# GpSimd makes the w2 sums of M1 and M3 one stage earlier, w2 tiles lie in column halves, and the M6/M7 differences overwrite g

## The chip, the cores and the metric

The kernel runs on one core of a Trainium2 chip. The metric is the device time of one execution in microseconds (us). It is measured over several executions on the chip; a profile of one execution gives a trace. The core has TensorE (PE; its weight loads are listed apart as PEld), VectorE (DVE), ScalarE (ACT), GpSimd (POOL) and SyncE (SP), whose queue here only issues DMAs.

## The reference, cut to what matters

```python
x  = randn(8, 1024, 1024); w1 = randn(1024, 4096); w2 = randn(4096, 1024)   # float32
h = x @ w1
h = 0.5 * h * (1 + np.tanh(np.sqrt(2 / np.pi) * (h + 0.044715 * h ** 3)))
out = (h @ w2).astype(np.float32)
```

## The kernel before

The 8192 rows are worked off in eight superblocks (sb 0 to 7) of 1024 rows. In each, the *first matmul* is x @ w1 with the activation, which leaves g in SBUF as four quarter blocks (g11, g12, g21, g22), and the *second matmul* is g @ w2. Each is a Strassen-like scheme: the operands are cut into 2 x 2 blocks and seven products M1 to M7 of sums and differences replace eight block products. The second matmul's products multiply these:

```python
B_TERMS = {1: ("11", SUB, "22"), 2: ("11", None, None), 3: ("12", ADD, "22"), 4: ("21", ADD, "11"),
           5: ("22", None, None), 6: ("11", ADD, "12"), 7: ("21", ADD, "22")}      # of w2
A_TERMS = {1: ("11", "22"), 2: ("21", "22"), 3: ("11", None), 4: ("22", None),
           5: ("12", "11"), 6: ("21", "11"), 7: ("12", "22")}                       # differences of g
```

A product can be run *one-level* (64 TensorE matmuls of 512 columns) or *two-level*: the same scheme is applied again inside the product, and 7 x 16 matmuls of 256 columns replace the 64. Two-level needs, besides the product's own operand of w2 (4 tiles), its four inner w2 sums. They are made once, stored to DRAM (`in_d`), and loaded by every later superblock. Superblocks 0 and 1 run everything one-level and store the sums of M2, M6 and M7. Superblock 2 runs M2, M6 and M7 two-level, and its second matmul makes the sums of M1 and M3 on VectorE while those products run one-level. Superblocks 3 to 7 run M1, M2, M3, M6 and M7 two-level, and M4 and M5 one-level.

What VectorE does between the products is a table; a key such as `51` means "after step 1 of M5":

```python
FILL_END = """;50:x621 x622;51:x611 a61;52:x612 a62;53:a63 a64
    ;61:x721;62:x722;63:x711;64:a71;65:x712;66:a72;67:a73
    ;71:a74;72:n5;73:n1;74:n2;75:n7;76:n6"""
FILL_2 = (
    dict(inner=(1, 2, 3, 6, 7), fill=slots("""00:x122 x112 a11 a12 a13 a14 x222 x212 ...""" + FILL_END)),
    dict(inner=(2, 6, 7), fill=slots("""00:g10 g11 g12 g13 x222 x212          # superblock 2
    ;10:a21 s11;11:a22 s12;12:a23 s13;13:a24 s14 s15
    ... ;30:s31;31:s32;32:s33;33:s34 s35""" + FILL_END)),
)
# x621: block 21 of M6's difference of g;  a61: M6's inner sum 1;  g10: M1's one-level difference;
# s11..s14: M1's inner w2 sums, s15: store plain quarters of M1's w2;  n5: a difference for the next x
```

`unit()` takes one of the 26 buffers (4 KB in each partition) that nearly everything shares: w1 and w2 tiles, differences, output sums.

```python
up = ctx.enter_context(tc.tile_pool(name="up", bufs=26))

def split_jobs(m, pieces):                     # inner w2 sums of product m
    ...
    def make(n):
        j, u, op, v = W_SUMS[n]
        t[n] = unit(NI // 2, OH // 2)
        for h in range(2):
            tt(t[n][:, h * QC:(h + 1) * QC, :], operand(u, h), operand(v, h), op, True)   # VectorE
        nc.gpsimd.dma_start(out=in_d[m][:, j - 1], in_=t[n])
    def plain():                               # the three quarters that are no sums: copied to DRAM
        for j, b in W_TERMS.items():
            for h in range(2):
                nc.gpsimd.dma_start(out=in_d[m][:, j - 1, h * QC:(h + 1) * QC, :], in_=operand(b, h))

class Inner:                                   # a two-level product
    def load(self):
        for j in W_ORDER:
            self.y[j] = unit(NI // 2, OH // 2)
            nc.sync.dma_start(out=self.y[j], in_=in_d[self.m][:, j - 1])
    def make_x(self, b):
        self.x[b] = unit(NI // 2, HT // 2)
        tt(self.x[b], inner_block(self.u, b), inner_block(self.v, b), SUB, True)

def matmul2(sb, g, early, nxt):
    order = (4, 1, 2, 3, 5, 6, 7)              # M4 first, M7 last
    ...
```

Output sums and M-products go to DRAM by DMAs that GpSimd issues; until such a store has read its tile, the tile's buffer is not free.

## Time and profile before

| | |
|---|---|
| time, 3 runs | median 1538.98 us (1538.09 to 1539.83) |
| span of the profiled run | 1538.1 us |
| TensorE busy | 1523.8 us, 99% |
| first matmul of sb 2, of sb 3 | 96.8, 96.7 us |
| second matmul of sb 2 | 99.5 us |
| second matmul of sb 3 to 6 | 89.1 us each |

TensorE is busy for 99% of the span, so only its own work and the gaps between its work matter. From the page of the kernel before, the busy times of the engines (us, share of the span, instructions):

```profile
PE 1523.8 (99%) x8606; PEld 844.5 (55%) x8606; DVE 1071.2 (70%) x1354; ACT 489.3 (32%) x821; POOL 330.7 (21%) x380
```

The windows view of the kernel before, cut at the stage boundaries that the chain of waits shows; the rows are the first and second matmul of superblock 2, then of superblock 3. Columns: the stretch, its length, then busy time and instructions of each engine, the granted clock of TensorE (1.00 is full), the DMA engines' mean busy share, and GB/s:

```profile
409.24:506.00 96.76, 96.76 (x450) 43.86 (x448) 57.41 (x84) 45.81 (x79) 16.45 (x20) 1.00 0.74 232
506.00:605.48 99.48, 94.16 (x593) 58.57 (x592) 69.41 (x82) 14.05 (x24) 29.66 (x43) 0.98 0.94 318
605.48:702.17 96.69, 96.69 (x449) 43.83 (x448) 55.18 (x81) 45.79 (x79) 22.61 (x18) 1.00 0.75 215
702.17:791.25 89.08, 88.92 (x690) 67.31 (x688) 72.66 (x82) 11.71 (x20) 16.43 (x21) 1.00 1.00 323
```

The two first matmuls are alike. Superblock 2's second matmul is 10.4 us longer than superblock 3's. Its TensorE is idle for 99.48 - 94.16 = 5.3 us, its mean clock is 0.98, and the rest of the difference is the one-level M1 and M3.

TensorE's timeline of that second matmul, from M5 on (start us, length, what; in brackets the idle time before it and who ended it):

```profile
559.50 13.98 PE L764 MATMUL ps<-u,gc 128*128 128x512 f16 x64
573.37 1.92 PE L699 MATMUL ps<-u 128*128 128x256 f16 x16
577.37 1.92 PE L699 MATMUL ps<-u,gc 128*128 128x256 f16 x16 [2.08 <-DVE gc L146]
579.13 1.91 PE L699 MATMUL ps<-u 128*128 128x256 f16 x16
581.97 3.65 PE L699 MATMUL ps<-u,gc 128*128 128x256 f16 x32 [0.93 <-DVE u L146]
585.46 1.91 PE L699 MATMUL ps<-u 128*128 128x256 f16 x16
589.68 2.78 PE L699 MATMUL ps<-u,gc 128*128 128x256 f16 x16 [2.31 <-DVE u L146]
592.25 2.75 PE L699 MATMUL ps<-u 128*128 128x256 f16 x16
594.84 1.91 PE L699 MATMUL ps<-u,gc 128*128 128x256 f16 x16
```

16 matmuls of 256 columns take 1.75 us start to start when nothing waits (as from 577.37 to 579.13); this is the *pitch*. The three marked groups start 4.00, 2.84 and 4.22 us after the group before them: 2.25, 1.09 and 2.47 us late, 5.8 us together. After the third, two groups of 16 take 2.57 and 2.59 us instead of 1.75: 1.7 us more. The windows view around it shows why:

```profile
587.00:590.40 3.40, 1.09 (x11) 0.83 (x9) 3.40 (x5) 0.00 (x0) 0.00 (x0) 1.00 1.02 414
590.40:594.00 3.60, 3.60 (x20) 2.60 (x19) 3.60 (x5) 0.00 (x0) 1.49 (x2) 0.53 0.86 281
594.00:597.00 3.00, 3.00 (x29) 2.70 (x28) 1.62 (x3) 0.59 (x1) 0.95 (x1) 1.00 0.99 191
```

From 590.4 to 594.0 the granted clock was 0.53 on average. What VectorE was doing before those gaps, from its timeline:

```profile
563.77 0.69 DVE L146 TENSOR_TENSOR u<-u,ps 128x512 f32<-128x512 f32 x1 [1.51 <-ACT tmp L159]
569.22 2.36 DVE L146 TENSOR_TENSOR u<-g,g 128x2048 f16<-128x2048 f16 x2 [4.76 <-DMA out_dram<-u]
...
573.23 1.22 DVE L146 TENSOR_TENSOR gc<-u 128x2048 f16<-128x2048 f16 x1
...
584.93 2.36 DVE L146 TENSOR_TENSOR u<-g,g 128x2048 f16<-128x2048 f16 x2 [3.02 <-DMA out_dram<-u]
587.21 0.68 DVE L146 TENSOR_TENSOR u<-tmp,ps 128x512 f32<-128x512 f32 x1
```

It sat idle for 4.76 us, and again for 3.02 us, until an output store had landed, and then made M6's and, from 584.93 on, M7's differences (`u<-g,g`), each in a buffer of its own. The inner sums (`gc<-u`) and the sum that empties a PSUM bank (`u<-tmp,ps`), for which TensorE waited, came after them in VectorE's order.

In the later superblocks one small gap is left in each second matmul. From the waits view of TensorE over superblocks 3 to 7:

```profile
PE ps L699 <- DVE u L146: 0.8, 5, 0.2
```

### The profile page before, as it was taken

The page shows a single profiled execution, that of the slowest core. Times are in us where ns is not written, and L with a number is a line of the kernel's source. Part 1 is how long each engine was busy: PE and PEld are TensorE (multiplying, and loading weights), DVE is VectorE, ACT ScalarE, POOL GpSimd, SP SyncE. Part 2 cuts the span into 40 slices and gives each one's busy share as a digit, 9 for nine tenths or more (in the row PEclk, how much of TensorE's full clock was granted, in tenths as well). Part 3 has the DMA queues.
Part 4 walks back from the last instruction along what each step waited for, and adds up shares of the span by engine and source line. Part 5 has one row for each costly group of instructions (what it writes and reads, how often), then busy time and mean ns, then how long its engine had stood idle before and what let it go on. Part 6 is the DMA issues. An engine that isn't in the chain of part 4 may idle for free.

```text
span 1538.1 us, 22679 instructions
## 1 busy us (share of the span) xinstructions
PE 1523.8 (99%) x8606; PEld 844.5 (55%) x8606; DVE 1071.2 (70%) x1354; ACT 489.3 (32%) x821; POOL 330.7 (21%) x380
## 2 busy tenths in 40 slices
PE   9999999999999999999999999999999999999998
PEld 5444444444444556446774467644775448744486
DVE  6876868768755567556875568755786566965677
ACT  6645024410244211442124421244113441144300
POOL 1242011212302241140211302122121310204011
PEclk9999999999999999999999999999999999999999
DMA  9999985994966799868997599966999669993696
GB/s 321 344 326 348 248 276 186 316 309 157 372 210 198 254 375 307 261 171 284 329 306 225 159 350 304 320 192 194 335 319 306 185 212 323 313 339 97 216 335 175
DMA packets 212654, 415.19 MB, mean 270 GB/s; under 512 B 77376, under 2 KB 84544, under 8 KB 211648
## 3 DMA queue, kind: packets, MB, share of 16 engines
q1 hardware_dynamic: 178560, 307.29, 59.2%
q0 software_dynamic: 33984, 106.45, 25.3%
q8 instruction: 67, 1.10, 0.3%
q14 instruction: 43, 0.35, 0.1%
HBM read 304.09 MB, written 124.26 MB: 278 GB/s over the span
## 4 chain that ended last, share of the span: by engine, by line
PE 90%; DMA 5%; DVE 2%; issue 1%; SPq 1%; ACT 0%; POOL 0%; DVEq 0%; POOLq 0%; ACTq 0%
PE ps L367 48%; PE ps L764 22%; PE ps L699 20%; DMA out_dram<-u 2%; DMA gc<-in_w_dram 2%; DVE u L146 1%; SPq L156 1%; DVE gc L146 1%; DMA u<-in_d 0%; DVE tmp L146 0%; DMA u<-in_x_dram 0%; ACT u L181 0%; POOL u L162 0%; ACT g L377 0%; POOL out_dram L478 0%
## 5 line engine op out<-in xcount | busy, mean ns | idle before, releaser
L367 PE MATMUL ps<-u 128*128 128x512 f16 x3584 | 776.2, 379 | 3.3 <-DVE tmp L146 1.7
L367 PEld LDWEIGHTS <-u 128*128 128x128 f16 x3584 | 350.5, 98 | 426.8 <-issue 4.9
L146 DVE TENSOR_TENSOR tmp<-tmp,ps 128x512 f32<-128x512 f32 x528 | 361.9, 687 | 296.4 <-ACT tmp L431 113.0
L377 ACT ACTIVATE g<-tmp 128x512 f16<-128x512 f32 x256 | 161.2, 630 | 293.6 <-DVE tmp L146 293.3
L764 PE MATMUL ps<-u,gc 128*128 128x512 f16 x1088 | 236.6, 379 | 0.0
L146 DVE TENSOR_TENSOR u<-u 128x2048 f16<-128x2048 f16 (+3 forms) x245 | 221.5, 933 | 15.8 <-ACT u L322 11.7
L699 PE MATMUL ps<-u,gc 128*128 128x256 f16 x1792 | 210.2, 273 | 6.1 <-DVE u L146 4.0
L699 PEld LDWEIGHTS <-gc 128*128 128x128 f16 x1792 | 175.6, 98 | 28.1 <-issue 5.3
L377 ACT ACTIVATE g<-ps 128x512 f16<-128x512 f32 x256 | 151.6, 596 | 88.7 <-PE ps L367 88.3
L764 PEld LDWEIGHTS <-gc 128*128 128x128 f16 x1088 | 106.4, 98 | 127.4
L764 PE MATMUL ps<-u,g 128*128 128x512 f16 x704 | 153.7, 379 | 0.0
L699 PE MATMUL ps<-u 128*128 128x256 f16 x1104 | 132.6, 274 | 0.0
L159 ACT COPY tmp<-ps 128x512 f32<-128x512 f32 x56 | 32.8, 586 | 274.0 <-PE ps L699 151.8
L146 DVE TENSOR_TENSOR u<-u,ps 128x512 f32<-128x512 f32 x129 | 88.4, 685 | 43.1 <-ACT tmp L159 19.1
L699 PEld LDWEIGHTS <-u 128*128 128x128 f16 x1104 | 108.4, 98 | 15.7 <-DVE u L146 0.4
L490 POOL DMA_DIRECT2D out_dram<-u x54 | 55.6, 1038 | 282.4 <-DVE u L146 263.3
L764 PEld LDWEIGHTS <-g 128*128 128x128 f16 x704 | 68.9, 98 | 82.9
L469 POOL TENSOR_TENSOR u<-g,g 128x2048 f16<-128x2048 f16 x22 | 89.2, 4065 | 81.7 <-ACT g L377 60.1
L431 ACT COPY tmp<-ps 128x512 f32<-128x512 f32 x128 | 72.9, 570 | 70.4 <-PE ps L367 69.7
L478 POOL DMA_DIRECT2D out_dram<-u x56 | 41.2, 764 | 240.8 <-ACT u L159 212.2
L146 DVE TENSOR_TENSOR tmp<-ps,tmp 128x512 f32<-128x512 f32 x128 | 88.4, 691 | 5.9 <-PE ps L367 1.2
L146 DVE TENSOR_TENSOR u<-g,g 128x2048 f16<-128x2048 f16 x70 | 83.5, 1220 | 11.3 <-DMA out_dram<-u 7.8
(40 smaller groups left out, 596.4 us busy)
## 6 DMA issues: line engine op xcount, KB each, us to landing
u<-in_d SPq DMA_DIRECT2D x196, 512.0 KB, 6.2
u<-w_d SPq DMA_DIRECT2D x240, 256.0 KB, 7.4
u<-raw_d SPq DMA_DIRECT2D x56, 512.0 KB, 6.4
out_dram<-u POOLq DMA_DIRECT2D x54, 512.0 KB, 9.9
gc<-in_w_dram SPq DMA_DIRECT2D x48, 512.0 KB, 6.1
u<-raw_d SPq DMA_DIRECT2D x96, 256.0 KB, 6.8
raw_d<-u SPq DMA_DIRECT2D x32, 512.0 KB, 9.8
w_d<-u POOLq DMA_DIRECT2D x32, 512.0 KB, 4.1
```

Of the source, the lines that this page charges most:

```text
L146: i = nc.vector.tensor_tensor(out=out, in0=in0, in1=in1, op=op)
L156: return tc.keep_in_program_order(nc.sync.dma_start(out=out, in_=in_, **kw))
L159: tc.keep_in_program_order(nc.scalar.copy(out=out, in_=in_))
L367: nc.tensor.matmul(bank, lhsT=ops[:, k, :], rhs=xs[m][:, k, :], start=(first and k == 0), stop=(k == KH - 1), skip_group_check=not first,)
L377: gelu_last[0] = nc.scalar.activation(out=g[b][:, c, :], in_=src, func=GELU)
L431: nc.scalar.copy(out=v, in_=pb)
L469: nc.gpsimd.tensor_tensor(out=early[m][b], in0=gu, in1=gv, op=SUB)
L478: return nc.gpsimd.dma_start(out=out2[r0:r0 + P, o0:o0 + OH], in_=src, **kw)
L490: return nc.gpsimd.dma_start(out=rows, in_=src, **kw)
L699: tc.keep_in_program_order(nc.tensor.matmul(bank[:, i * OH // 2:(i + 1) * OH // 2], lhsT=t[:, c, i * P:(i + 1) * P], rhs=self.y[j][:, c, : ...
L764: i = nc.tensor.matmul(bank, lhsT=a[:, c, :], rhs=pieces[c // QC][:, c % QC, :], start=(first and c == 0), stop=(c == NI - 1), skip_group_ ...
```

## The change

The intent: superblock 2 becomes like the later ones. GpSimd, which has time in superblock 2's first matmul, loads the operands of M1 and M3 there and makes their sums. w2 tiles are laid out in column halves, so that a quarter of a stored operand is one contiguous row of 2 KB and the plain quarters need no copies in `in_d`. M6's and M7's differences are written over g's own blocks, take no buffers, and are made earlier. The diff, cut to its core:

```diff
+IN_PLACE = (6, 7)
-FILL_END = """;50:x621 x622;51:x611 a61;52:x612 a62;53:a63 a64
-    ;61:x721;62:x722;63:x711;64:a71;65:x712;66:a72;67:a73 ...
-FILL_2 = (dict(inner=(1, 2, 3, 6, 7), ...), dict(inner=(2, 6, 7), ... s11 ... s35 ...))
+FILL_2 = slots("""00:x122 x112 a11 a12 a13 a14 x222 x212 x622 x612 x621 x611
+    ...
+    ;50:a61 x721;51:a62 x722;52:a63 x711;53:a64 x712
+    ;64:a71;66:a72;67:a73;71:a74;72:n5;73:n1;74:n2;75:n7;76:n6""")
 ...
+            if sb == 2 and c < 8 and c % 2 == 0:                  # in the first matmul
+                split_on_pool(FROM_SUMS[c // 4], c // 2 % 2)
 ...
-            sums[m] = raw[over] if over else [unit(QC, OH) for _ in range(NI // QC)]
+            sums[m] = raw[over] if over else [unit(2, HALF) for _ in range(NI // QC)]
 ...
-        def plain():
-            for j, b in W_TERMS.items(): ...
+    def split_on_pool(m, h):
+        raw = []
+        for k in range(2):
+            raw.append(unit(2, HALF))
+            nc.sync.dma_start(out=flat(raw[k]), in_=stored(w2_d[2 * k + h], raw2_d[2 * k + h], m))
+        for n, (_, u, op, v) in W_SUMS.items():
+            ...
+            nc.gpsimd.tensor_tensor(out=t[n], in0=in0, in1=in1, op=op)
+            nc.gpsimd.dma_start(out=in_d[m][:, n - 1, h * QC:(h + 1) * QC, :] ..., in_=t[n])
 ...
     def load(self):
         for j in W_ORDER:
             self.y[j] = unit(NI // 2, OH // 2)
-            nc.sync.dma_start(out=self.y[j], in_=in_d[self.m][:, j - 1])
+            if j not in W_TERMS: ...                              # a sum: from in_d, as before
+            for h in range(2):                                    # a plain quarter: from the stored operand
+                nc.sync.dma_start(out=self.y[j][:, h * QC:(h + 1) * QC, :] ..., in_=d[:, b * HALF:(b + 1) * HALF])
     def make_x(self, b):
-        self.x[b] = unit(NI // 2, HT // 2)
+        self.x[b] = inner_block(self.u, b) if self.m in IN_PLACE else unit(NI // 2, HT // 2)
 ...
             i = nc.tensor.matmul(
-                bank, lhsT=a[:, c, :], rhs=pieces[c // QC][:, c % QC, :], ...
+                pair(bank), lhsT=a[:, c, :], rhs=chunks(pieces[c // QC])[:, :, c % QC, :], ...
```

More of the change, by code (lines that the diff above doesn't have):

```diff
@@ L52 @@
 FROM_2 = (2,)
-INNER = MADE_INNER + FROM_2 + (1, 3)
+FROM_SUMS = (1, 3)
+INNER = MADE_INNER + FROM_2 + FROM_SUMS
+IN_PLACE = (6, 7)
 ORDER = (4, 5, 1, 2, 3, 7, 6)
@@ L58 @@
     {(3, 2): 1, (3, 3): 2, (6, 0): 2, (6, 1): 1, (6, 2): 2, (6, 3): 2},
-    {(7, 2): 1, (7, 3): 1, (3, 0): 2, (3, 1): 1, (3, 2): 1, (3, 3): 2, (6, 0): 1, (6, 1): 1, (6, 2): 2, (6, 3): 3},
+    {(7, 2): 1, (7, 3): 1, (3, 0): 1, (3, 1): 1, (3, 2): 1, (3, 3): 2, (6, 0): 1, (6, 1): 1, (6, 2): 2, (6, 3): 2},
 )
@@ L72, in slots @@
     return {(int(k[0]), int(k[1])): v.split() for k, v in (row.split(":") for row in table.split(";"))}
-FILL_END = """;50:x621 x622;51:x611 a61;52:x612 a62;53:a63 a64
-    ;61:x721;62:x722;63:x711;64:a71;65:x712;66:a72;67:a73
-    ;71:a74;72:n5;73:n1;74:n2;75:n7;76:n6""".replace("\n    ", "")
-FILL_2 = (
-    dict(inner=(1, 2, 3, 6, 7), fill=slots("""00:x122 x112 a11 a12 a13 a14 x222 x212
+FILL_2 = slots("""00:x122 x112 a11 a12 a13 a14 x222 x212 x622 x612 x621 x611
     ;12:a21;14:a22;15:a23;17:a24
     ;21:u0 u1;22:a31;23:u2 u3;24:a32;25:a33 d11;26:d22;27:a34 d21 d12
-    ;32:g50;34:g51 e11;35:g52 e22;36:e21;37:g53 e12""".replace("\n    ", "") + FILL_END)),
-    dict(inner=(2, 6, 7), fill=slots("""00:g10 g11 g12 g13 x222 x212
-    ;10:a21 s11;11:a22 s12;12:a23 s13;13:a24 s14 s15
-    ;21:u0 u1;22:g50;23:u2 u3;24:g51;25:g52 d11;26:d22;27:g53 d21 d12
-    ;30:s31;31:s32;32:s33;33:s34 s35""".replace("\n    ", "") + FILL_END)),
-)
+    ;32:g50;34:g51 e11;35:g52 e22;36:e21;37:g53 e12
+    ;50:a61 x721;51:a62 x722;52:a63 x711;53:a64 x712
+    ;64:a71;66:a72;67:a73;71:a74;72:n5;73:n1;74:n2;75:n7;76:n6""".replace("\n    ", ""))
 @with_exitstack
@@ L114 @@
     QW = QC * P
+    HALF = QC * OH // 2
     up = ctx.enter_context(tc.tile_pool(name="up", bufs=26))
@@ L131 @@
     raw_d = [dram.tile([P, 4, KH * QW], DT, name=f"raw_d{q}") for q in range(NI // QC)]
-    in_d = {m: dram.tile([P, 7, NI // 2, OH // 2], DT, name=f"in_d{m}") for m in INNER}
+    in_d = {m: dram.tile([P, 4, NI // 2, OH // 2], DT, name=f"in_d{m}") for m in INNER}
     w2_d = [dram.tile([P, 7, QC * OH], DT, name=f"w2_d{q}") for q in range(NI // QC)]
@@ L148, in tt, with chunks @@
             tc.keep_in_program_order(i)
+    def chunks(t):
+        return t.rearrange("p o (c n) -> p o c n", c=QC)
     def flat(t):
@@ L268, in load_pieces @@
         for q in range(NI // QC):
-            pieces.append(unit(QC, OH))
+            pieces.append(unit(2, HALF))
             nc.sync.dma_start(out=flat(pieces[q]), in_=stored(w2_d[q], raw2_d[q], m))
@@ L465, in matmul1 @@
                 m, b = EARLY[c - NI + 4]
-                if m in FILL_2[sb == 2]["inner"]:
-                    early[m][b] = unit(NI // 2, HT // 2)
-                    gu, gv = (inner_block(g[t], b) for t in A_TERMS[m])
-                    nc.gpsimd.tensor_tensor(out=early[m][b], in0=gu, in1=gv, op=SUB)
+                early[m][b] = unit(NI // 2, HT // 2)
+                gu, gv = (inner_block(g[t], b) for t in A_TERMS[m])
+                nc.gpsimd.tensor_tensor(out=early[m][b], in0=gu, in1=gv, op=SUB)
         finish(*late)
@@ L504, in bring @@
                 for b in bs:
-                    t = unit(QC, OH)
+                    t = unit(2, HALF)
                     raw[b].append(t)
@@ L512, in bring @@
                         cast_in(
-                            t[:, j:j + 2, :],
+                            chunks(t)[:, :, j:j + 2, :],
                             w2v[int(b[1]) - 1, int(b[0]) - 1, :, c:c + 2, :],
@@ L516, in bring @@
                             staged,
+                            view=lambda st: st.rearrange("p c (o n) -> p o c n", o=2),
                         )
@@ L534, in add @@
             tt(t, raw[u][q], raw[v][q], op, m != 4)
-            if sb and m not in MADE_INNER:
-                nc.gpsimd.dma_start(out=w2_d[q][:, m - 1, :], in_=flat(t))
+            if sb:
+                n = HALF if m in MADE_INNER and q < 2 else 2 * HALF
+                nc.gpsimd.dma_start(out=w2_d[q][:, m - 1, :n], in_=flat(t)[:, :n])
         def pieces(m):
@@ L640, in operand @@
             k, b = int(v[0]) - 1, int(v[1]) - 1
-            return pieces()[2 * k + h][:, :, b * OH // 2:(b + 1) * OH // 2]
+            return chunks(pieces()[2 * k + h])[:, b]
         def make(n):
-            j, u, op, v = W_SUMS[n]
+            _, u, op, v = W_SUMS[n]
             t[n] = unit(NI // 2, OH // 2)
@@ L647, in make @@
                 tt(t[n][:, h * QC:(h + 1) * QC, :], operand(u, h), operand(v, h), op, True)
-            nc.gpsimd.dma_start(out=in_d[m][:, j - 1], in_=t[n])
-        def plain():
-            for j, b in W_TERMS.items():
-                for h in range(2):
-                    nc.gpsimd.dma_start(out=in_d[m][:, j - 1, h * QC:(h + 1) * QC, :], in_=operand(b, h))
-        return [lambda n=n: make(n) for n in W_SUMS] + [plain]
+            nc.gpsimd.dma_start(out=in_d[m][:, n - 1], in_=t[n])
+        return [lambda n=n: make(n) for n in W_SUMS]
+    def split_on_pool(m, h):
+        raw = []
+        for k in range(2):
+            raw.append(unit(2, HALF))
+            q = 2 * k + h
+            nc.sync.dma_start(out=flat(raw[k]), in_=stored(w2_d[q], raw2_d[q], m))
+        t = {}
+        for n, (_, u, op, v) in W_SUMS.items():
+            if n % 2:
+                two = unit(2, HALF)
+            t[n] = two[:, (n + 1) % 2]
+            in0, in1 = (
+                t[b] if isinstance(b, int) else raw[int(b[0]) - 1][:, int(b[1]) - 1] for b in (u, v)
+            )
+            nc.gpsimd.tensor_tensor(out=t[n], in0=in0, in1=in1, op=op)
+            nc.gpsimd.dma_start(
+                out=in_d[m][:, n - 1, h * QC:(h + 1) * QC, :].rearrange("p c n -> p (c n)"), in_=t[n]
+            )
     def inner_block(t, b):
@@ L680, in load @@
                 self.y[j] = unit(NI // 2, OH // 2)
-                nc.sync.dma_start(out=self.y[j], in_=in_d[self.m][:, j - 1])
+                if j not in W_TERMS:
+                    n = next(n for n in W_SUMS if W_SUMS[n][0] == j)
+                    nc.sync.dma_start(out=self.y[j], in_=in_d[self.m][:, n - 1])
+                    continue
+                k, b = (int(d) - 1 for d in W_TERMS[j])
+                for h in range(2):
+                    d = stored(w2_d[2 * k + h], raw2_d[2 * k + h], self.m)
+                    nc.sync.dma_start(
+                        out=self.y[j][:, h * QC:(h + 1) * QC, :].rearrange("p c n -> p (c n)"),
+                        in_=d[:, b * HALF:(b + 1) * HALF],
+                    )
         def make_x(self, b):
-            self.x[b] = unit(NI // 2, HT // 2)
+            self.x[b] = inner_block(self.u, b) if self.m in IN_PLACE else unit(NI // 2, HT // 2)
             tt(self.x[b], inner_block(self.u, b), inner_block(self.v, b), SUB, True)
@@ L764, in matmuls2 @@
             i = nc.tensor.matmul(
-                bank,
+                pair(bank),
                 lhsT=a[:, c, :],
-                rhs=pieces[c // QC][:, c % QC, :],
+                rhs=chunks(pieces[c // QC])[:, :, c % QC, :],
                 start=(first and c == 0),
@@ L793, in matmul2 @@
     def matmul2(sb, g, early, nxt):
-        inner = FILL_2[sb == 2]["inner"]
-        fill = FILL_2[sb == 2]["fill"]
         end = sb == NSB - 1
-        ops, pieces, splits = {}, {}, {}
+        ops, pieces = {}, {}
         u2, u = halves()
@@ L822, in post4 @@
             store(sb, "21", q, u[q])
-        def post1(q, ps):
-            act_copy(rows[1][q], ps)
-        def post3(q, ps):
-            d = rows[1][q]
-            store(sb, "12", q, copy(q, ps))
-            tt(d, d, ps, ADD, True)
-            store(sb, "22", q, d)
         def post5(q, ps):
@@ L837, in post5 @@
                 store(sb, "11", q, u[q])
-        posts = {1: post1, 3: post3, 4: post4, 5: post5}
+        posts = {4: post4, 5: post5}
         def load(m):
-            if m in inner:
+            if m in products:
                 products[m].load()
@@ L847, in run @@
         def run(key):
-            for job in fill.get(key, ()):
+            for job in FILL_2.get(key, ()):
                 kind, m, i = job[0], int(job[1]), job[2:]
@@ L855, in run @@
                     ops[m, int(i)] = operand2(g, m, int(i), True)
-                elif kind == "s":
-                    if m not in splits:
-                        splits[m] = split_jobs(m, lambda: pieces[m])
-                    splits[m].pop(0)()
                 elif kind == "u":
@@ L877, in matmul2 @@
                 load(after)
-            if m in inner or m == 1:
+            if m in products:
                 into[m], rows[m] = halves()
-            if m in inner:
                 for n in products[m].steps(into[m]):
```

## The prediction

> **What bounds the kernel now.** The page's busy table has TensorE at 1523.8 of 1538.1 us (99%) at full clock; VectorE 70%, GpSimd 21%. Only its work and gaps count. By the chain of waits, each superblock's first matmul takes 96.7 us without a gap. The second takes 89.1 us in superblocks 3 to 6, but 99.5 us in superblock 2 (506.0 to 605.5): 10.4 us more. TensorE's timeline and waits explain it:
> - M1 and M3 are 64 matmuls of 512 columns (13.81 us each); later superblocks' two-level form is 112 of 256 columns (336 take 36.68 us: 12.23 us each): 2 x 1.58 = 3.2 us.
> - TensorE idles 5.3 us (2.08, 0.93, 2.31) at M6's and M7's start, waiting for VectorE. VectorE itself waited 7.8 us for output stores to free the buffers of the M6/M7 differences, and M1's and M3's w2 sums share its queue.
> - After the last gap 32 matmuls take 0.16 us instead of 0.109 us, granted clock 0.89 in that slice: 1.7 us. The Trainium skill, "TensorE: Matmul & The Clock Gate", Part 1, says an idle window re-gates the clock and about 3.4 us of activity reopens it; the trace agrees in kind.
>
> In superblocks 3 to 7 the waits view shows five gaps of 0.16 us in M6: 0.8 us.
>
> **What the change does.** Superblock 2 runs M1 and M3 two-level too. GpSimd makes their 16 sums (128x1024, estimated 2.1 us each from 4.07 us for 128x2048: about 34 us, plus 0.54 us per store issue) in superblock 2's first matmul, where it is busy 16 of 97 us. VectorE's sums and the plain copies' stores go; stored w2 is read in column halves instead. M6's and M7's differences overwrite g: eight buffers fewer; M6's four are made during M4, M7's during M5.
>
> **What lies on the critical path.** All of the 10.4 us, if the stage becomes like superblock 3's, and most of the 0.8 us. The added work should not: the first matmul moves about 8 MB more (4 loaded, 4 stored) on 22.5 MB. Its DMA share is full until about 440 us, but 0.23 and 0.44 in 445 to 469, with w1 pieces loaded ahead. GpSimd's sums delay the next x's casts and transposes by perhaps 10 to 15 us, within slack. VectorE's operations there read one SBUF tensor and PSUM; the skill's "SBUF — State Buffer" says GpSimd and VectorE exclude each other only for two SBUF inputs or a two-port mode. Strided right-hand sides (two runs of 256 columns) should cost nothing, nor half-size loads: 2 KB rows move as fast in the trace.
>
> **Prediction.** 1539.0 - 10.4 - 0.8 = 1527.8, so 1528; 80% range 1525.5 to 1533.0. Faster by over 2%: 0.01; within 2%: 0.98; slower: 0.01.
>
> **What would show it.** Windows: superblock 2's second matmul about 89 us, VectorE there near 72 us, no TensorE wait over 0.3 us, no slice at lower clock; its first matmul still 96.7 us, with GpSimd near 55 us and DMA share near 1. M4/M5 spacing still 215.8 ns.
>
> **What would make it wrong.** A gap in superblock 2's first matmul, from w1 pieces queued behind w2 loads or late transposes; M1's or M3's sums reaching memory late; M6's early differences delaying VectorE at M1 (about 14 us of work in M4's 13.8 us); GpSimd's w2 casts slowing with the half layout before 119 us (about 2 us of slack); a cost per strided matmul (1 ns on 1792 would be 1.8 us).

## The result, and the profile after

| | before | after |
|---|---|---|
| time | 1539.12 us (1538.09 to 1539.83, 4 runs) | 1528.11 us (1527.93 to 1528.69, 4 runs) |
| span of the profiled run | 1538.1 us | 1525.9 us |
| first matmul of sb 2 | 96.8 us | 96.8 us |
| second matmul of sb 2 | 99.5 us | 88.8 us |
| second matmul of sb 3 | 89.1 us | 88.8 us |

The ratio is 0.993 (95% interval 0.9912 to 0.9947). Ratios here are the mean time of one kernel's fast runs over that of the other's of the same rounds, so not quite the ratio of the medians. The unaltered changed kernel ran again at 1528.61 us beside 1540.13 us of the kernel before (ratio 0.9928).

The page of the changed kernel, and the windows view over the same four stages:

```profile
PE 1517.1 (99%) x8702; PEld 852.3 (56%) x8702; DVE 1073.8 (70%) x1354; ACT 486.3 (32%) x817; POOL 357.2 (23%) x380
```

```profile
409.20:506.02 96.82, 96.82 (x450) 43.82 (x448) 57.38 (x84) 45.80 (x79) 65.55 (x52) 1.00 0.92 298
506.02:594.78 88.76, 88.76 (x690) 67.31 (x688) 72.90 (x82) 11.70 (x20) 16.51 (x21) 1.00 1.00 323
594.78:691.48 96.70, 96.70 (x450) 43.86 (x448) 55.14 (x81) 45.79 (x79) 22.65 (x18) 1.00 0.76 222
691.48:780.24 88.76, 88.76 (x689) 67.32 (x688) 72.91 (x82) 11.70 (x20) 16.42 (x21) 1.00 1.00 322
```

TensorE's busy time equals each stage's length: no gap is left in any of the four. GpSimd is busy 65.6 us instead of 16.5 in superblock 2's first matmul, the DMA share there rose from 0.74 to 0.92, and the stage has the same length as before. VectorE's busy time in that stage did not change (57.4 us). The chain of waits of the changed kernel (start us, length, what) is matmuls end to end from superblock 1 on; its middle:

```profile
409.20 96.82 PE ps L366 x448
506.02 13.81 PE ps L791 x64
519.84 36.68 PE ps L726 x336
556.52 13.81 PE ps L791 x64
570.33 24.45 PE ps L726 x224
594.78 96.69 PE ps L366 x448
```

M4 and M5 are the `x64` pieces, 13.81 us as before, although their right-hand side is now two runs of 256 columns; M1 to M3 are the 336 matmuls of 36.68 us, M6 and M7 the 224 of 24.45 us. The sum is 88.76 us in superblock 2 as in the later ones. The whole list of TensorE's waits for VectorE, ScalarE or DMAs after the change is this, all of it at the start of the kernel (before 50 us):

```profile
PE ps L366 <- DVE tmp L142: 1.5, 2, 1.4
PE ps L366 <- DVE u L142: 1.4, 1, 1.4
PE ps L295 <- DVE warm L906: 1.2, 1, 1.2
PE ps L366 <- ACT tmp L430: 0.6, 1, 0.6
```

In the profiled pair the stages account for the difference: 99.48 - 88.76 = 10.72 us in superblock 2's second matmul, five times 89.08 - 88.76 = 1.6 us in the later ones, 0.07 us given back in superblock 2's first: 12.25 us, against spans that differ by 12.2 us. The medians differ by 11.0 us. The profiled run of the kernel before took 1539.93 us, more than any of the four runs in the table; that of the changed kernel, 1527.93 us, is its fastest. The runs of the kernel before scatter more (1537.8 to 1542.8 us over all calls) than those of the changed kernel (1527.9 to 1529.2 us).

GpSimd's timeline in superblock 2's first matmul after the change, one of the four rounds of sums:

```profile
422.10 2.12 POOL L669 TENSOR_TENSOR u<-u 128x1024 f16<-128x1024 f16 x1 [0.49 <-DMA u<-w_d]
...
425.12 4.22 POOL L669 TENSOR_TENSOR u<-u 128x1024 f16<-128x1024 f16 x2
429.27 1.10 POOL L670 DMA_DIRECT2D in_d<-u  x2
430.39 2.13 POOL L669 TENSOR_TENSOR u<-u 128x1024 f16<-128x1024 f16 x1
...
433.50 1.01 POOL L337 DMA_DIRECT2D xb<-in_x_dram  x2
```

A sum of 128x1024 took 2.12 us, a round with its stores 11.3 us, and the next cast of x (`xb<-in_x_dram`) came at 433.5 us instead of 433.0. The four rounds ran from 422.1 to 470.7 us.

### The profile page after: what moved, and what is told of

Read it like the earlier page. It is cut to its first block, busy times and chain, and to the rows that moved or that the text cites. A ratio compares the mean times of both kernels' runs of the same rounds, so it can differ in the third digit from the quotient of the medians.

```text
span 1525.9 us, 22990 instructions
## 1 busy us (share of the span) xinstructions
PE 1517.1 (99%) x8702; PEld 852.3 (56%) x8702; DVE 1073.8 (70%) x1354; ACT 486.3 (32%) x817; POOL 357.2 (23%) x380
## 4 chain that ended last, share of the span: by engine, by line
PE 85%; DVE 0%; issue 0%
PE ps L366 44%; PE ps L726 24%; PE ps L791 17%; DVE u L142 0%
## 5 line engine op out<-in xcount | busy, mean ns | idle before, releaser
L366 PEld LDWEIGHTS <-u 128*128 128x128 f16 x3584 | 350.5, 98 | 427.1 <-issue 4.7
L726 PE MATMUL ps<-u,gc 128*128 128x256 f16 x1920 | 224.3, 273 | 0.0
L142 DVE TENSOR_TENSOR u<-u 128x2048 f16<-128x2048 f16 (+3 forms) x233 | 211.9, 937 | 16.6 <-ACT u L321 11.7
L791 PE MATMUL ps<-u,gc 128*128 128x512 f16 x1024 | 222.6, 379 | 0.0
L726 PEld LDWEIGHTS <-gc 128*128 128x128 f16 x1920 | 187.9, 98 | 21.7
L791 PEld LDWEIGHTS <-gc 128*128 128x128 f16 x1024 | 100.1, 98 | 119.6
L791 PE MATMUL ps<-u,g 128*128 128x512 f16 x640 | 139.8, 379 | 0.0
L469 POOL TENSOR_TENSOR u<-g,g 128x2048 f16<-128x2048 f16 x24 | 97.2, 4067 | 75.0 <-ACT g L376 60.1
L791 PEld LDWEIGHTS <-g 128*128 128x128 f16 x640 | 62.7, 98 | 75.5
L726 PE MATMUL ps<-u,g 128*128 128x256 f16 x864 | 103.1, 273 | 0.0
L726 PEld LDWEIGHTS <-g 128*128 128x128 f16 x864 | 84.5, 98 | 11.1
L142 DVE TENSOR_TENSOR u<-tmp,ps 128x512 f32<-128x512 f32 x60 | 41.3, 688 | 63.9 <-PE ps L726 41.4
```

The source lines that it names most:

```text
L142: i = nc.vector.tensor_tensor(out=out, in0=in0, in1=in1, op=op)
L366: nc.tensor.matmul(bank, lhsT=ops[:, k, :], rhs=xs[m][:, k, :], start=(first and k == 0), stop=(k == KH - 1), skip_group_check=not first,)
L469: nc.gpsimd.tensor_tensor(out=early[m][b], in0=gu, in1=gv, op=SUB)
L726: tc.keep_in_program_order(nc.tensor.matmul(bank[:, i * OH // 2:(i + 1) * OH // 2], lhsT=t[:, c, i * P:(i + 1) * P], rhs=self.y[j][:, c, : ...
L791: i = nc.tensor.matmul(pair(bank), lhsT=a[:, c, :], rhs=chunks(pieces[c // QC])[:, :, c % QC, :], start=(first and c == 0), stop=(c == NI ...
```

## The experiments

The rival readings were these. *Buffers*: the gaps came because the M6/M7 differences waited for output stores to free buffers. *Queue*: they came because VectorE had M1's and M3's sums to make in the same stage. Besides, which part of the change is worth what, and how near the new work in the first matmul is to doing harm. "Second matmul" below is always that of superblock 2, read from the chain of waits and the windows view. Each call of four runs also timed the kernel before on the same chip (medians 1540.11, 1539.80, 1540.13 us). The intervals of the ratios are about 0.0015 to either side, 2.3 us, so differences of 2 us between variants do not rest on the totals; they rest on the stage times of the profiles.

| run | median us | ratio to before (95%) | second matmul of sb 2 |
|---|---|---|---|
| before | 1539.1 to 1540.1 | | 99.5 |
| in_place_only | 1534.63 | 0.9966 (0.9951 to 0.9981) | 93.2 |
| layout_only | 1534.88 | 0.9969 (0.9954 to 0.9984) | 93.8 |
| stores_back_pool | 1539.94 | 0.9999 (0.9984 to 1.0014) | 99.6 |
| stores_back_act | 1543.60 | 1.0026 (1.0011 to 1.0041) | 101.8 |
| sums_on_pool_only | 1534.03 | 0.9962 (0.9948 to 0.9977) | 92.3 |
| two_level_only | 1529.97 | 0.9939 (0.9921 to 0.9956) | 89.1 |
| in_place_old_slots | 1530.47 | 0.9940 (0.9925 to 0.9955) | 89.1 |
| changed kernel, again | 1528.61 | 0.9928 (0.9911 to 0.9944) | 88.8 |
| sums_on_vector | 1530.44 | 0.9937 (0.9920 to 0.9954) | 88.8 |
| pool_twice | 1559.16 | 1.0127 (1.0112 to 1.0142) | 91.8 |
| two_level_24 | 1555.14 | 1.0100 (1.0085 to 1.0115) | 92.9 |
| after_24 | 1581.83 | 1.0274 (1.0258 to 1.0289) | 98.0 |

All gave correct results.

### The changed kernel again

No edit; it ran beside sums_on_pool_only and the two runs with fewer buffers.

> The changed kernel unaltered, for comparison on the same chip as the others of this call: ratio 0.993 to the kernel before, second matmuls 88.76 us.

Ratio 0.9928, and 88.77 us for the second matmul: the result repeats.

### In place alone

```diff
 # the kernel before
-            self.x[b] = unit(NI // 2, HT // 2)
+            self.x[b] = inner_block(self.u, b) if self.m in (6, 7) else unit(NI // 2, HT // 2)
```

> The kernel before, with only this: the M6 and M7 differences overwrite g, at their old places in the order of VectorE's work. Superblock 2 keeps M1 and M3 one-level with VectorE making their w2 sums. Theory B (buffers: VectorE was late because the tiles of the differences waited 7.8 us for output stores): the three TensorE gaps (2.25, 1.09 and 2.47 us over the pitch) and the slow clock after them (1.7 us) vanish, superblock 2's second matmul takes 92 us instead of 99.5, total about 1531.6 us. Rival Q (VectorE's queue is full of M1's and M3's sums): the gaps stay, stage 98 us or more, total 1538 or more. Under both, the M6 gap of superblocks 3 to 7 stays (stage 89.1).

The second matmul took 93.2 us. VectorE's 16 sum operations for M1 and M3 are still there, and the long gaps are gone: TensorE's waits there are one of 0.16 us and one of 0.93 us at the boundary to the next superblock, for a w1 piece. VectorE waits for no output store any more in this stage. The stores themselves are as slow as before: the one whose landing ended the first long wait of the kernel before took 14.74 us from issue to landing there, and its counterpart here, issued at 553.92 us, 14.71 us. Only nothing waits for it now. That is *buffers*, and *queue* falls. The 92 us that were expected had left out that 0.93 us, and the total, 1534.63 us, is 3.0 us above the one expected: 1.2 us of it lie in this stage, 1.1 us in the kernel before, whose median was 1540.11 us in this call; the rest was not pursued.

### Two-level and the sums on GpSimd, without in place

```diff
 # the changed kernel
-IN_PLACE = (6, 7)
+IN_PLACE = ()
-FILL_2 = ... x622 x612 x621 x611 ... ;50:a61 x721;51:a62 x722;52:a63 x711;53:a64 x712 ...
+FILL_2 = ... ;50:x621 x622;51:x611 a61;52:x612 a62;53:a63 a64;61:x721;62:x722;63:x711;64:a71;65:x712 ...
```

> The changed kernel without its in-place part: differences in buffers of their own, made at the old places. Superblock 2 runs M1 and M3 two-level with sums by GpSimd. If superblock 2 then simply becomes like superblock 3 of the kernel before: its second matmul 89.1 us, no wait over 0.3 us, M6 gap stays in all six superblocks (0.32 us over the pitch each), total about 1.9 us over the changed kernel, 1530.0 us. If the buffers are what matters in superblock 2 even so, gaps of over 1 us at M6 or M7 return there and it takes over 91 us.

As expected to the tenth: 89.08 us, 1529.97 us. So superblock 2 gets all of its 10.4 us without the in-place part, and the in-place part, with its earlier places, is worth the 0.32 us of each of six second matmuls.

### In place, at the old positions in VectorE's order

```diff
 # the changed kernel; IN_PLACE = (6, 7) stays
-FILL_2 = ... x622 x612 x621 x611 ... ;50:a61 x721;51:a62 x722;52:a63 x711;53:a64 x712 ...
+FILL_2 = ... ;50:x621 x622;51:x611 a61;52:x612 a62;53:a63 a64;61:x721;62:x722;63:x711;64:a71;65:x712 ...
```

> The changed kernel with the in-place differences put back to their old places in the order of VectorE's work (M6's during M5, M7's during M6). If the M6 gap of the later superblocks comes from the order (VectorE has differences queued ahead of a sum that frees a PSUM bank), it is back in all six: stage 89.1 us, total about 1530.0 us. If it came from buffers, it stays away: 88.8 us, 1528.1 us.

The M6 gap is back in all six second matmuls (six waits of 0.16 us shown, stages of 89.08 us, 1530.47 us). The small gap was one of order: VectorE had differences queued ahead of the sum that frees a PSUM bank. Writing in place does not cure it; making the differences earlier does. That the earlier places need the in-place writing, because M6's four tiles would otherwise take four of the 26 buffers so early, is argued and was not run.

### The layout alone

```diff
 # the changed kernel, with IN_PLACE = () and the old positions, and in superblock 2:
-                split_on_pool(FROM_SUMS[c // 4], c // 2 % 2)
+# M1 and M3 one-level; their sums on VectorE in the second matmul, at the old places:
+    ;10:a21 s11;11:a22 s12;12:a23 s13;13:a24 s14 ... ;30:s31;31:s32;32:s33;33:s34
```

> The changed kernel with M1 and M3 of superblock 2 one-level again, their sums by VectorE in the second matmul as before, differences in own buffers at old places: what is left of the change is the column-half layout, the strided right-hand sides and the plain quarters loaded from stored w2. Expected: as the kernel before, 1539 us within 1.5 us; one-level product still 13.81 us, first matmul stages 96.7 us. If dropped stores of the plain copies relieve the output stores of superblock 2, its gaps shrink and the total falls by up to 3 us. If strided right-hand sides cost 1 ns, the total rises by 1.8 us.

This missed: 1534.88 us, 5.2 us below the kernel before, where at most 3 were allowed for. The one-level product still took 13.81 us, so the strided right-hand sides cost nothing. But the gaps shrank to two, and the slow clock vanished. The first line is VectorE's, where the kernel before had waited 4.76 us:

```profile
565.13 2.36 DVE L151 TENSOR_TENSOR u<-g,g 128x2048 f16<-128x2048 f16 x2 [0.33 <-DMA out_dram<-u]
...
579.22 3.65 PE L734 MATMUL ps<-u,gc 128*128 128x256 f16 x32 [0.16 <-DVE u L151]
...
586.03 1.91 PE L734 MATMUL ps<-u,gc 128*128 128x256 f16 x16 [1.41 <-DVE u L151]
```

In that stage VectorE waited 2.4 us for output stores instead of 7.8. The only thing that this version removes there is 3.1 MB of stores, the plain quarters of M1 and M3. The next two runs put them back.

### The plain stores put back, from GpSimd and from ScalarE

```diff
 # layout_only
+        def plain():
+            for b in W_TERMS.values():
+                for h in range(2):
+                    nc.gpsimd.dma_start(out=scratch[m][...], in_=operand(b, h))   # or nc.scalar
-    ... 13:a24 s14 ... 33:s34
+    ... 13:a24 s14 s15 ... 33:s34 s35
```

> layout_only with the plain copies of M1's and M3's w2 quarters (3.1 MB) stored again in superblock 2's second matmul, by GpSimd as before, to a scratch tensor nobody reads. If their bytes on the DMA engines, or their place in GpSimd's queue ahead of the output stores, made the buffers come free late, the long gaps are back: superblock 2's second matmul 97 us or more against 93.8 of layout_only, VectorE waiting over 5 us for output stores, total about 1538 to 1540 us. If layout_only gained by something else (loads by halves, the M2 and sb-1 stores), it stays at 93.8 us and 1535 us.

> The same scratch stores issued by ScalarE instead of GpSimd. If the bytes matter, as with GpSimd: 97 us or more. If it is GpSimd's queue[...], as layout_only: 93.8 us, 1535 us. ScalarE has 85 us idle in that stage; a wait for a loaded piece there could itself delay PSUM copies, which would show as TensorE waits for ACT.

The gaps are back in both. With GpSimd they have the sizes of the kernel before:

```profile
577.71 1.92 PE L743 MATMUL ps<-u,gc 128*128 128x256 f16 x16 [2.08 <-DVE gc L152]
...
582.31 3.65 PE L743 MATMUL ps<-u,gc 128*128 128x256 f16 x32 [0.93 <-DVE u L152]
...
589.99 3.54 PE L743 MATMUL ps<-u,gc 128*128 128x256 f16 x16 [2.28 <-DMA u<-in_d]
```

The third is put down to a load (`u<-in_d`); VectorE's sum before it ended 0.05 us earlier, so both were late. VectorE's waits for output stores (from the waits views of this stage: total, times, longest) in the kernel before, in layout_only, and with the stores back from GpSimd and from ScalarE:

```profile
DVE u L146 <- DMA out_dram<-u: 7.8, 2, 4.8
DVE u L151 <- DMA out_dram<-u: 2.4, 2, 2.1
DVE u L152 <- DMA out_dram<-u: 8.0, 2, 5.0
DVE u L152 <- DMA out_dram<-u: 9.9, 2, 6.3
```

Two other readings are open at this point: the plain stores could hold up the issue of the output stores, or they could themselves keep buffers from coming free. The traces settle it. The output store whose landing ended VectorE's first wait was issued at nearly the same time in all four, at 554.45, 554.79, 554.59 and 555.27 us, and landed after 14.74, 10.31, 14.88 and 13.55 us. So it is the bytes on the DMA engines, not GpSimd's queue, and not buffers held by the plain stores. The engines are full either way: the DMA share from 542 to 590 us is 1.05 in the kernel before and in layout_only alike. What differs is how long an output store takes: 11.0 to 13.6 us from issue to landing before, 8.9 to 10.6 us in layout_only (medians of the three kinds in that stretch). With ScalarE the third gap grew to 5.6 us and the clock was low twice as long; why that variant is worse than GpSimd's was not pursued.

### The sums moved to GpSimd, M1 and M3 still one-level

```diff
 # layout_only
-    ;10:a21 s11;11:a22 s12;12:a23 s13;13:a24 s14 ... ;30:s31;31:s32;32:s33;33:s34
+    ;10:a21;11:a22;12:a23;13:a24 ...
+                split_on_pool(FROM_SUMS[c // 4], c // 2 % 2)      # in the first matmul
```

> Between layout_only and two_level_only: the 16 sums are made by GpSimd in superblock 2's first matmul, but M1 and M3 of its second matmul stay one-level, differences in own buffers at the old places. By the accounts of the two neighbours, two-level itself is worth 2 x 1.58 us of matmul work and nothing else: second matmul 89.08 + 3.16 = 92.2 us, against 93.8 of layout_only (the rest of the gap goes) and 89.1 of two_level_only; total about 1533.2 us. If two-level also changes when buffers come free, it differs from 92.2 by over 0.5 us.

92.26 us. The remaining large gap is gone, VectorE waits for no output store, and 92.26 - 89.08 = 3.18 us is left for two-level, the 3.16 us of matmul work and nothing else. Why the gap is gone has more than one possible reason, since with the sums their eight tiles and the 4.2 MB of their stores left the stage too: the DMA share from 542 to 590 us fell to 0.94, and the output store followed above landed after 6.69 us. No run separates these.

### The same sums on VectorE in the first matmul

```diff
 # the changed kernel, split_on_pool
-            nc.gpsimd.tensor_tensor(out=t[n], in0=in0, in1=in1, op=op)
+            nc.vector.tensor_tensor(out=t[n], in0=in0, in1=in1, op=op)
```

> The changed kernel with the 16 sums in superblock 2's first matmul made by VectorE instead of GpSimd (0.65 us each, about 10 us in a stage where VectorE is busy 57 of 97 us). If VectorE's free time is what counts, the total stays at 1528 us. If the order counts (a burst of three or four sums, or a wait for its load, ahead of a PSUM read that the next product needs), TensorE gets gaps of 0.5 to 2 us at the four bursts: first matmul 98.5 to 103 us, total 1530 to 1534 us.

The first matmul took 98.9 us instead of 96.8; TensorE's timeline has two gaps there:

```profile
453.50 10.74 PE L366 MATMUL ps<-u 128*128 128x512 f16 x49 [0.92 <-DVE tmp L142]
465.07 45.05 PE L366 MATMUL ps<-u 128*128 128x512 f16 x208 [0.83 <-DVE tmp L142]
```

VectorE had 39 us free in that stage and needs only 9 more (66.3 us busy instead of 57.4). It is the order that costs: three sums in a row, 1.9 us, and a wait for their load stand ahead of a PSUM read that the next product needs. GpSimd takes three times as long for a sum (2.12 us against 0.69), but has no PSUM read in its order that the sums could hold up, and with it the stage is as long as in layout_only, which has no sums there (96.82 us in both). The total, 1530.44 us, is 1.8 to 2.3 us above the changed kernel's two medians. They were run at other times.

### Each GpSimd sum made twice

```diff
 # the changed kernel, split_on_pool
+            for _ in range(2):
-            nc.gpsimd.tensor_tensor(out=t[n], in0=in0, in1=in1, op=op)
+                nc.gpsimd.tensor_tensor(out=t[n], in0=in0, in1=in1, op=op)
```

> The changed kernel with each of the 16 GpSimd sums made twice (the same result written again): GpSimd about 99 us busy in a stage of 97. Reading of the slack from the trace: the last cast of the next x moves from 458 to about 484 us, the transposes from 467 to about 492, and the last w1 half queued behind the first four of them lands about 507, needed at 494; so a TensorE gap of 8 to 16 us in the first matmul, total 1536 to 1545 us. If the prefetch hides even this, 1528 us.

The direction was right, the size was too small: TensorE waits 20.3 us for the last w1 half, then 4.4 us for the first w2 piece of M4, and runs at half speed after both.

```profile
514.13 15.84 PE L366 MATMUL ps<-u 128*128 128x512 f16 x60 [20.29 <-DMA u<-w_d]
534.33 6.03 PE L792 MATMUL ps<-u,g 128*128 128x512 f16 x14 [4.36 <-DMA u<-w_d]
```

The last cast of x went out at 501.5 us, not at 484, because it stood behind all of the doubled rounds in GpSimd's order, and the transposes that wait for it stand ahead of the last w1 half in SyncE's. In the changed kernel the first transpose goes out at 467.1 us, 4.8 us later than before, without effect. So the free place for GpSimd's sums is real but not large: between 34 and 68 us of sums it ends.

### Two buffers fewer

```diff
 # the changed kernel (after_24), and two_level_only (two_level_24)
-    up = ctx.enter_context(tc.tile_pool(name="up", bufs=26))
+    up = ctx.enter_context(tc.tile_pool(name="up", bufs=24))
```

> two_level_only (differences in own buffers) with 24 buffers. By the buffer theory of the gaps, its M6/M7 differences must now wait for output stores in every superblock from 2 on: second matmuls 91 us or more instead of 89.1, total 1540 us or more. If buffers are not what held VectorE in the kernel before, it stays near 1530 us.

> The changed kernel with the big pool cut from 26 to 24 buffers. If the in-place part leaves buffers to spare (eight tiles fewer in a second matmul), second matmuls stay at 88.8 us and the total within 1.5 us of the changed kernel, any loss being in first matmuls, whose w1 halves run ahead less. If it has no spare, gaps of over 0.5 us in the second matmuls, total 1533 us or more.

Without in place, M6's and M7's differences wait for output stores again in five of the six second matmuls, and TensorE has its gap of 2 to 2.8 us with them: the *buffers* reading, produced on purpose. But the changed kernel suffers more: of the second expectation, the branch "no spare" came, and far beyond the 1533 us named there. VectorE's timeline in after_24, at M6's first step of superblock 2:

```profile
573.66 1.22 DVE L142 TENSOR_TENSOR g<-g,g 128x2048 f16<-128x2048 f16 x1
582.53 0.69 DVE L142 TENSOR_TENSOR u<-tmp,ps 128x512 f32<-128x512 f32 x1 [7.66 <-DMA out_dram<-u]
```

Now the tile of M6's own output sum (`u<-tmp,ps`) waits 7.7 us for a store, and TensorE is idle up to 8.2 us in each second matmul but the last. The eight buffers that the in-place part frees do not seem to lie idle: M7's w2 loads stand earlier in the program than that tile and were all issued by 574 us in after_24; that they took the freed buffers is read from this order, not shown by a run of its own. With 22 buffers the program deadlocks when it is simulated, and it was not run; with more than 26 it does not fit into SBUF, so the direct test "the kernel before with more buffers" could not be made.

## Why the prediction was right

- **Size and range.** 1528.0 us was predicted, 1528.11 us measured, within 1525.5 to 1533.0, and "within 2%" (0.7%). That the two agree to 0.1 us is partly luck. 10.4 + 0.8 = 11.2 us was predicted; the profiled pair shows 10.7 + 1.6 us less 0.07 us, 12.25 us, because the M6 gap is twice as large as predicted and goes in superblock 2 too. The predicted 11.2 us were taken off the median (1538.98 us), though they were read from a profiled run of 1539.93 us. The two errors, 1.05 us and 0.95 us, nearly cancel.
- **"All of the 10.4 us, if the stage becomes like superblock 3's".** Shown: 88.76 us in both. The three terms stand singly: 3.18 us for two-level (sums_on_pool_only against two_level_only), 5.8 us of gaps and 1.7 us at half clock, which come and go together with VectorE's waits for output stores.
- **The cause of the gaps.** The prediction named two, the buffers held by stores and the sums in VectorE's queue (and put the third gap at M7's start; it is M6's last step, held by M7's differences). in_place_only leaves the sums and loses the gaps, so the first is enough. What the prediction did not see is why the stores were late: the plain copies' 3.1 MB on DMA engines that were already full. It listed those stores as merely gone. Two parts of the change, in place and no plain stores, each cure all or most of the gaps alone, 6.3 and 5.7 us of the stage; the sums moved away, run only on top of the second, bring it to 7.2 us. Together they give no more than the gap there was.
- **"Five gaps of 0.16 us: 0.8 us".** The mechanism was right and the term was mis-sized by half. The waits view counts a gap from the modelled end of the matmul before, which includes its drain; start to start the loss was 0.32 us (955.58 to 957.65 is 2.07 us instead of 1.75), so 1.6 us.
- **GpSimd's load.** "Near 55 us" was 65.6: the sums took 34 us as estimated (16 of 2.13 us), but two more early differences of M1 (8.1 us) and 16 store issues (9 us) were not added up. It did not matter: the delay of the next x was 4.8 us, less than the 10 to 15 feared.
- **The added work off the critical path.** Shown by 96.82 us against 96.76 in the first matmul. pool_twice shows that this had an end, and sums_on_vector that the choice of engine mattered.
- **The dangers named.** None came: M4's spacing is unchanged, GpSimd's w2 casts still take 1.04 us each, and VectorE, with M6's differences in M4's time, was idle for 2.1 us before M1's first sum needed it.

The skill's page "TensorE: Matmul & The Clock Gate", Part 1, helped to place the 1.7 us: it describes a clock that is either full or half and is set by windows of 3.4 us. The trace agrees: one low stretch, granted 0.50 for 3.41 us, 0.213 us per 256-column matmul in it instead of 0.109. "SBUF — State Buffer" (section "SBUF: two separate sides") says that GpSimd excludes VectorE only when VectorE uses two SBUF inputs or a two-port mode. Of VectorE's 84 operations in the first matmul, 80 take one operand from PSUM. The prediction overlooked the other four (sums of two SBUF tiles), but they are over by 413 us, before GpSimd's sums start at 422.1 us. VectorE's busy time did not move (57.41 to 57.38 us) with 49 us more work on GpSimd, so this agrees as far as it goes; no run here put sums of two SBUF inputs against each other on purpose.

## What to carry to other kernels

These are readings of this one kernel. When a vector engine is late, ask first what its next output tile waits for: a buffer held by a store on full DMA engines looks, from the matmul's side, just like an overloaded queue, and removing bytes, removing tiles or removing work may each cure the same gap, so their gains do not add. Work that reads no PSUM did best here on an engine that no PSUM bank waits for, though that engine is three times slower, as long as what stands behind it in its queue has time to spare. Eight tiles fewer left no two buffers to spare here, so count the slack by taking buffers away on the chip, not by counting tiles.

## What the Trainium skill lacked or had wrong

- "TensorE: Matmul & The Clock Gate" (Back-to-back issue gap) says that streams of weight load and matmul pairs sustain about 131 ns for 512 columns and that N/2.4 + 2.5 ns over-counts there. Here such a stream ran at 13.81 us / 64 = 215.8 ns for 512 columns and 36.68 us / 336 = 109.2 ns for 256, exactly the formula (215.8 and 109.2 ns), over whole stages.
- The same page (Part 1, and its table of goals) puts the limit for a harmful gap at about 3 to 3.4 us of idle time. Here a gap of 2.31 us (as shown in the timeline) was followed by a stretch at half clock (granted 0.53 from 590.4 to 594.0 us). In two_level_24 a gap of 2.69 us was not, and one of 2.10 us was (16 matmuls shown as 3.19 us instead of 1.91): the length of the gap alone does not decide. The page says that its windows run freely, so the place of the gap in them may; no run here tests that.
- "GPSIMD Engine Reference" (3.1 and 4.1) measures a two-input elementwise operation on GpSimd for fp32 only, and gives it as about 2 times slower than VectorE. For float16 the runs show 4.07 us against 1.22 us for 128x2048 (3.3 times) and 2.12 us against 0.69 us for 128x1024 (3.1 times).
- No page was found that says how a wait view's idle time relates to lost matmul time: 0.16 us shown was 0.32 us lost start to start.
